# Banks of the s5 read-out and of the gelu's transposes taken from the heads' pool

## The chip, the cores and the metric

The kernel runs on one core of one Trainium2 chip. The metric is the device time of one execution in microseconds (us); lower is better. All times below are from that core.

## What is computed

One inference step of a decoder layer: 2,048 prompt tokens with 16 meta tokens ahead of them, and 8 single sampled tokens. The reference, cut to the part in which the change lies:

```python
def block(h, ...):
    hn = rms_norm(h, norm_mix_g)
    z = hn @ w_in
    u, q, fl, iv, g = ...
    y5, s5r, s5i = s5_mix(u, ...)
    yh, hg = hgrn_mix(q, fl, iv, g, ...)
    h = h + jnp.concatenate([y5, yh], axis=-1) @ w_out
    yf, conv = conv_ffn(rms_norm(h, norm_ffn_g), ...)
    return h + yf, ...

def s5_mix(u, ...):
    xr = jnp.einsum('nlgc,gpc->nlgp', ug, bbr)
    xi = jnp.einsum('nlgc,gpc->nlgp', ug, bbi)
    ...
    _, _, hr, hi = lax.associative_scan(_complex_scan_op, (a_r, a_i, xr, xi), axis=1)
    y = (jnp.einsum('nlgp,gcp->nlgc', hr, c_re) - jnp.einsum('nlgp,gcp->nlgc', hi, c_im))
    y = y.reshape(n, l, S5_DIM) + d * uf
    y = jax.nn.gelu(y)
    y = y * jax.nn.sigmoid(y @ w_glu + b_glu)
    return y, hr[:, -1], hi[:, -1]
```

`hgrn_mix` is a gated linear recurrence of four heads in chunks of 64 tokens; its matrix state goes from chunk to chunk.

## The kernel before

The prompt is cut into four blocks of 512 tokens (b = 0 to 3); the meta and sampled tokens ride with block 0. Dense products are made in three passes of split fp32 (high and low parts of weights and activations): `fm_mm` (matmul L480) for features by tokens, `tm_mm` (L500) for the heads' v and gate, `tm_wide` (L520) for the output projection. Each weight unit is loaded by SP into `st`, split by ACT (`wh`, L449) and DVE (`wl`, L83), two stages and three splits deep.

For each block `head` runs for h = 0 to 3: the forget gate's projection (L480), a running product and its reciprocal on DVE, q's projection, v and gate (L500), then the attention of the head on PE: scores (L723), transposed keys (L729), state increments (L734), output (L746, L747), with the state update on DVE between (L743, L80). The transposes of the finished head (L768, in `tail`) are put off to the next head by the list `PEND`, which `flush` empties after the next projection. After the heads, `u_proj` projects u, which goes to DRAM and comes back in the layout of s5 as tile `U` (by SP, L839, and, for the tokens of block 0's extras, by POOL, L842 and L845).

The s5 mixer of block b - 1 runs in eight units `bt`, two ahead of each head of block b (four ahead of the first two heads of the last block). A unit's chain is: increments on PE (L896) into a bank `tp`; a swap of its halves by ACT (L272, L273) and products on DVE (L86, L80); a scan on DVE (L934); swap, products and a subtraction again (L86, L83); the read-out on PE (L948, with the direct part L945 on U), copied by ACT into `sY` (L954). Units of block 0 also carry the extra tokens: L906, L919 to L929, L960, L963, L968. After the second unit of a pair, `s5_finish` (put off through `PEND` as well) makes the gelu (L86, L853, ACT L855, L856), transposes it on PE (L863, L872) and splits it (ACT L866, DVE L867).

PSUM has eight banks of 128x512 fp32, in three pools: `ps` with three (`bank`, name `mm`), `pt` with two (`tbank`, name `tp`), `pg` with three (`gbank`, name `hg`). A tile framework orders the instructions of each engine: it gives out a pool's banks in the order in which the program asks for them, and an instruction whose bank isn't free yet comes later in its engine's queue. So the pool that a bank comes from decides what may be placed ahead of what. In the program's order a pair of units asks first (increments, read-out), then the flush inside the head (tail of the head before, finish of the pair), then the head's scores, keys and increments.

Of the kernel before, what the change touches and what calls it, by code (L numbers as in the profile page):

```python
# [37 lines left out]
def kernel(  # L38
# [52 lines left out]
    def tbank():  # L91
        return pt.tile([128, 512], F32, name="tp")

    def gbank():
        return pg.tile([128, 512], F32, name="hg")
# [14 lines left out]
    def v3(t, a, b):  # L110
        return t[:, :a * b].rearrange("p (a b) -> p a b", a=a)
# [374 lines left out]
    def behind(ins, prev):  # L486

        if prev is not None:
            tc.add_manual_dep(ins.ins, prev.ins.name, mybir.DependencyInfo(
                mybir.DependencyClass.NoSync, mybir.DependencyReason.DATA), reason="bank shared by groups")  # L490
        return ins
# [88 lines left out]
    def put_cols(a, src, ks, lo, n):  # L580

        hi = a[0][:, ks, lo:lo + n]
        nc.vector.tensor_copy(hi, src)
        sub(a[1][:, ks, lo:lo + n], src, f_(hi))
# [263 lines left out]
    def gelu2(y, m):  # L848

        q = s5p.tile([128, 516], F32, name="sB")[:m, :512]  # L850
        yy = y[:m]
        mul(q, yy, yy)
        ts_(q, q, 0.044715, 1.0, op0=OP.mult, op1=OP.add)  # L853
        mul(q, q, yy)
        ACT(q, q, AF.Tanh, scale=GELU_C)  # L855
        stt(yy, q, 1.0, yy, op0=OP.add, op1=OP.mult)  # L856

    def s5_finish(b, bt, Y, ye, m):
        ft = bt // 2
        gelu2(Y.rearrange("p a b -> p (a b)"), 128)  # L860
        p = v3(tbank(), 4, 128)
        for t in range(4):
            nc.tensor.transpose(p[:, t, :], Y[:, t, :], ident)  # L863
        hi = m[0][:, 4 + ft, 0:BT].rearrange("p (j t) -> p t j", t=4)
        lo = m[1][:, 4 + ft, 0:BT].rearrange("p (j t) -> p t j", t=4)
        ACT(hi, p, AF.Copy, scale=0.5)  # L866
        stt(lo, p, 0.5, f_(hi), op0=OP.mult, op1=OP.subtract)  # L867
        if b == 0:
            gelu2(ye.rearrange("p a b -> p (a b)"), 9)
            p = v3(tbank(), 3, 16)  # L870
            for i, t in enumerate((0, 2, 3)):
                nc.tensor.transpose(p[:, i, 0:9], ye[:9, t, :], ident[:9, :9])  # L872
            tm = sm.tile([128, 10], F32, name="yx", bufs=2)
            ts_(tm[:, 0:2], p[:, 1:3, 0], 0.5, None, op0=OP.mult)
            ts_(tm[:, 2:10], p[:, 0, 1:9], 0.5, None, op0=OP.mult)
            put_cols(m, tm[:, None, :], slice(4 + ft, 5 + ft), FM_, 10)

    def s5(b, ut, m, bts, later=None):
        for bt in bts:
# [59 lines left out]
            mul(Gw, Gw, St)  # L939
            sub(G, G, Gw)  # L940
            nc.vector.tensor_copy(Hc[:, 4 * bt:4 * bt + 4], G[:, :, 128])
            py = v3(tbank(), 4, 64)
            o = None
            for i in range(2):
                behind(mm(py[:, 2 * i:2 * i + 2, :].rearrange("p a b -> p (a b)"), UT[:, i, 0:128], T[:, i, :],  # L945
# [8 lines left out]
            ACT(Y[:, :, 64 * half:64 * half + 64].rearrange("p t (g c) -> p g t c", c=16),  # L954
                py.rearrange("p g (t c) -> p g t c", c=16), AF.Copy)
            if b == 0:
                pye = v3(tbank(), 4, 64)
                o = None
                for i in range(2):
                    behind(mm(pye[:9, 2 * i:2 * i + 2, :].rearrange("p a b -> p (a b)"),  # L960
                              UT[:, i, 131:140], T[:, i, :], start=True, stop=False), o)
                    for j in range(2):
                        o = mm(pye[:9, 2 * i:2 * i + 2, :].rearrange("p a b -> p (a b)"), he[:, 2 * i + j, :],  # L963
                               Cm[:, 2 * i + j, :], start=False, stop=(j == 1))
                if half == 0:
                    E["ye"] = s5p.tile([128, 4, 128], F32, name="sY")
                ye = E["ye"]
                ACT(ye[:9, :, 64 * half:64 * half + 64].rearrange("p t (g c) -> p g t c", c=16),  # L968
                    pye[:9].rearrange("p g (t c) -> p g t c", c=16), AF.Copy)
            if half == 1:  # L970
                fin = lambda m, bt=bt, Y=Y, ye=E.get("ye"): s5_finish(b, bt, Y, ye, m)
                if later is None:
                    PEND.append(lambda fin=fin: fin(m))
                else:
                    later.append(fin)
# [119 lines left out]
    for b in range(NB):  # L1095
# [4 lines left out]
        for h in range(4):  # L1100
            if last and h == 2:
                U[b] = u_proj(b, A[b])
                fin = []
                stage_out(b - 1, lambda q: s5(b, U[b], None, (q,), fin))
                M[b] = new_act(b)
                mix_split(b, M[b], MIX[b])
                for f in fin:
                    f(M[b])
            if last and h < 2:
                s5(b - 1, U[b - 1], M[b - 1], range(4 * h, 4 * h + 4))  # L1110
            elif last:
                s5(b, U[b], M[b], (2 * h, 2 * h + 1))
            elif b > 0:
                s5(b - 1, U[b - 1], M[b - 1], (2 * h, 2 * h + 1))
            MIX[b].append(head(b, A[b], h))
            if b == 0 and h == 0:
                s5_factors()
                setup = s5_setup()
                next(setup)
            if b == 0 and h == 1:  # L1120
                next(setup, None)
            if b == 0 and h == 2:
                norm1(1)
# [234 lines left out]
```

## Time and profile before

| what | us |
|---|---|
| median of 3 runs (2536.32 to 2539.64) | 2537.81 |
| the profiled execution | 2535.7 |
| its span, first to last instruction | 2534.0 |
| PE busy in it | 2445.5 |
| DVE busy in it | 1453.3 |
| ACT busy in it | 902.6 |

Busy time is the union of an engine's instructions; that of PE holds the overlapping tails of matmuls that follow each other. The times of the rows below count from the span's start. The heads and s5 take about the first 1,000 us, the ConvFFN the rest.

### The profile page before, as it was taken

What the parts mean: (1) busy time and instruction counts of PE and PEld (TensorE: products, weight loads), DVE (VectorE), ACT (ScalarE), POOL (GpSimd) and SP (SyncE); (2) the same over time, 40 slices, a digit from 0 to 9 for tenths busy, and PEclk for the clock granted to TensorE, in tenths of its full rate; (3) what the DMA queues carried; (4) which work ended last, traced back from release to release, by engine and by line L of the source; (5) the groups of instructions that cost most, each with busy time, mean ns of one, the idle gap of its engine ahead of it and who ended that gap; (6) DMA issues with size and microseconds to landing.
All of it is one profiled execution on the core that took longest, in us unless ns stands there. A gap on an engine that the chain in (4) does not pass through costs nothing.

```text
span 2534.0 us, 33854 instructions
## 1 busy us (share of the span) xinstructions
PE 2445.5 (97%) x13515; PEld 2088.5 (82%) x13515; DVE 1453.3 (57%) x2950; ACT 902.6 (36%) x1548; POOL 166.6 (7%) x252
## 2 busy tenths in 40 slices
PE   7989899999999989999999999999999999999998
PEld 6878787788888778888989898988788888888886
DVE  6897788688678688553343434445843433343344
ACT  3554445344435444432313131323531313131222
POOL 2223001000100001000000000000400000000000
PEclk9999999999999999999999999999999999999999
DMA  4357435543564555531111111111621111111112
GB/s 126 103 159 205 114 101 141 191 142 127 148 215 158 162 164 192 170 92 43 50 44 48 47 45 42 46 55 59 211 66 50 44 48 50 50 50 50 34 54 80
DMA packets 251260, 252.13 MB, mean 99 GB/s; under 512 B 11303, under 2 KB 208751, under 8 KB 246998
## 3 DMA queue, kind: packets, MB, share of 16 engines
q1 hardware_dynamic: 241088, 220.42, 28.8%
q0 software_dynamic: 9840, 29.48, 3.6%
q8 instruction: 106, 1.74, 0.3%
q14 instruction: 52, 0.43, 0.1%
q10 hardware_dynamic: 174, 0.06, 0.0%
HBM read 216.41 MB, written 33.27 MB: 99 GB/s over the span
## 4 chain that ended last, share of the span: by engine, by line
PE 72%; DVE 11%; issue 4%; ACT 3%; DMA 1%; POOL 1%; SPq 0%; POOLq 0%; ACTq 0%; DVEq 0%
PE mm L480 42%; PE mm L1282 9%; PE hg L1282 9%; PE mm L500 3%; PE hg L520 3%; PE mm L520 2%; DVE sB L86 2%; DVE sA L934 1%; DVE wl L83 1%; DVE sA L86 1%; PE mm L539 1%; DVE hf L665 1%; POOL rstd L546 1%; DMA x<-h_d 1%; PE tp L572 1%
## 5 line engine op out<-in xcount | busy, mean ns | idle before, releaser
L480 PE MATMUL mm<-ah,wh 128*128 128x512 f32 (+3 forms) x2312 | 811.6, 351 | 5.9 <-ACT ah L577 3.3
L480 PE MATMUL mm<-al,wh 128*128 128x512 f32 (+3 forms) x2312 | 810.8, 351 | 1.1 <-DVE al L83 1.1
L480 PE MATMUL mm<-ah,wl 128*128 128x512 f32 (+3 forms) x2312 | 810.8, 351 | 1.0 <-DVE wl L83 1.0
L449 ACT ACTIVATE wh<-st 128x1024 fp32r<-128x1024 f32 (+1 forms) x264 | 276.4, 1047 | 709.2 <-PE mm L480 298.0
L83 DVE TENSOR_TENSOR wl<-st,wh 128x1024 fp32r<-128x1024 f32 (+1 forms) x264 | 318.4, 1206 | 350.4 <-ACT wh L449 348.4
L480 PEld LDWEIGHTS mm<-ah,wh 128*128 128x128 f32 x2312 | 438.9, 190 | 59.7 <-ACT ah L577 3.9
L480 PEld LDWEIGHTS mm<-ah,wl 128*128 128x128 f32 x2312 | 438.7, 190 | 56.2 <-issue 1.6
L480 PEld LDWEIGHTS mm<-al,wh 128*128 128x128 f32 x2312 | 438.1, 189 | 54.8 <-DVE al L83 1.6
L86 DVE TENSOR_TENSOR c<-c,mm 128x512 f32<-128x512 f32 (+1 forms) x110 | 63.6, 580 | 211.7 <-PE mm L480 210.3
L500 PE MATMUL mm<-wh,ah 128*128 128x256 f32 x512 | 146.3, 286 | 3.0 <-DVE hP L86 1.7
L500 PE MATMUL mm<-wl,ah 128*128 128x256 f32 x512 | 144.8, 284 | 1.7 <-DVE wl L83 1.7
L500 PE MATMUL mm<-wh,al 128*128 128x256 f32 x512 | 145.9, 285 | 0.0
L1282 PE MATMUL mm<-wh,gh 128*128 128x512 f32 x352 | 137.4, 390 | 0.0
L1282 PE MATMUL hg<-wh,gl 128*128 128x512 f32 x352 | 137.1, 390 | 0.0
L1282 PE MATMUL hg<-wl,gh 128*128 128x512 f32 x352 | 137.1, 390 | 0.0
L1282 PE MATMUL mm<-wh,gl 128*128 128x512 f32 x352 | 137.1, 389 | 0.0
L1282 PE MATMUL mm<-wl,gh 128*128 128x512 f32 x352 | 137.1, 389 | 0.0
L1282 PE MATMUL hg<-wh,gh 128*128 128x512 f32 x352 | 137.0, 389 | 0.0
L80 DVE TENSOR_TENSOR hacc<-hacc,hg 128x512 f32<-128x512 f32 x96 | 65.8, 686 | 88.2 <-PE hg L1282 87.7
L1220 ACT ACTIVATE c<-c 128x512 f32<-128x512 f32 x88 | 55.6, 632 | 144.8 <-DVE c L1219 144.8
L80 DVE TENSOR_TENSOR hacc<-hacc,mm 128x512 f32<-128x512 f32 x96 | 65.7, 685 | 66.0 <-PE mm L1282 65.8
L500 PEld LDWEIGHTS mm<-wh,ah 128*128 128x128 f32 x512 | 97.7, 191 | 4.7 <-DVE hP L86 2.5
(406 smaller groups left out, 3569.0 us busy)
## 6 DMA issues: line engine op xcount, KB each, us to landing
st<-in_ffn_w_up_dram SPq DMA_DIRECT2D x96, 512.0 KB, 3.8
big<-tab_d SPq DMA_DIRECT2D x32, 1156.0 KB, 5.4
st<-in_w_in_dram SPq DMA_DIRECT2D x48, 512.0 KB, 5.0
st<-in_ffn_w_down_dram SPq DMA_DIRECT2D x40, 512.0 KB, 3.5
st<-in_w_in_dram SPq DMA_DIRECT2D x64, 256.0 KB, 3.1
st<-in_w_out_dram SPq DMA_DIRECT2D x32, 512.0 KB, 3.6
x<-in_x_prompt_dram SPq DMA_DIRECT2D x30, 512.0 KB, 5.0
h_d<-x POOLq DMA_DIRECT2D x16, 512.0 KB, 4.2
```

What stands on the lines that cost most here:

```text
L80: tt_(o, a, b, op=OP.add)
L83: tt_(o, a, b, op=OP.subtract)
L86: tt_(o, a, b, op=OP.mult)
L449: ACT(hi[:, :n], st[:, :n], AF.Copy)
L480: mm(p[:, :n], w[wi][:, k, :], a[ai][:, k, c0:c0 + n], start=(i == 0), stop=(i == 3 * nk - 1))
L500: o = mm(dst, lhs(ai, k), (hi, lo)[wi][:, kk, :], start=(i == 0), stop=(i == tot - 1))
L520: mm(pb[t], lhs(ai, k, t), wu[wi][:, kk, :], start=(k == 0 and j == 0), stop=(k == 7 and j == 2))
L539: mm(dst[:m], stat[:, k, :m], w[:, kk, :], start=(i == 0), stop=(i == tot - 1))
L546: nc.gpsimd.tensor_tensor(r, r, mhalf[:ss.shape[0], :n], op=OP.pow)
L572: nc.tensor.transpose(p[:, k, :], x[:, kk * 128:kk * 128 + 128], ident)
L1220: ACT(c, c, AF.Silu)
L1282: mm(ps_[t], gs[b, f0 + k][ai][:, t * 128:t * 128 + 128], wus[i][wi][:, kk, :], start=(k == 0 and j == 0), stop=(k == nf - 1 and j == 2))
```

## The change

The read-out banks (`py`, and `pye` of block 0's extra tokens) and the two banks of the gelu's transposes come from `pg`, the pool of the heads' attention, in place of `pt`. The increments keep `pt` for themselves.

```diff
     def s5_finish(b, bt, Y, ye, m):
         ft = bt // 2
         gelu2(Y.rearrange("p a b -> p (a b)"), 128)
-        p = v3(tbank(), 4, 128)
+        p = v3(gbank(), 4, 128)
         for t in range(4):
             nc.tensor.transpose(p[:, t, :], Y[:, t, :], ident)
...
             gelu2(ye.rearrange("p a b -> p (a b)"), 9)
-            p = v3(tbank(), 3, 16)
+            p = v3(gbank(), 3, 16)
...
-            py = v3(tbank(), 4, 64)
+            py = v3(gbank(), 4, 64)
...
             if b == 0:
-                pye = v3(tbank(), 4, 64)
+                pye = v3(gbank(), 4, 64)
```

What it does to the order of the queues is shown at three places.

PE at the first head of block 1, before: after the last L500 of head 0 the head's attention follows, then the next projection (mm_3084 is the bank of head 0's v and gate, hP and hk its decayed queries and keys).

```order
L500 MATMUL mm_3084<-wl_3028,ah_1734 128x256
L723 MATMUL hg_3135<-hP_2968,hk_2966 128x128 x4
L729 MATMUL hg_3143<-ident_111,hk_2966 128x128 x4
L746 MATMUL mm_3154<-hv_3031,att_3140 128x128
L747 MATMUL mm_3154<-Sp_3155,hP_2968 128x128
L734 MATMUL hg_3149<-hv_3031,hf_2935 128x128 x4
L746 MATMUL mm_3154<-hv_3031,att_3140 128x128
L480 MATMUL mm_3340<-ah_1734,wh_3336 128x512
```

The same place now (big_2756 is the table of unit 0, big_2831 that of unit 1; sA holds a unit's scan, he its extra states):

```order
L500 MATMUL mm_3084<-wl_3028,ah_1734 128x256
L896 MATMUL tp_2760<-U_2472,big_2756 128x148 x2
L896 MATMUL tp_2761<-U_2472,big_2756 128x148 x2
L945 MATMUL hg_2813<-big_2756,U_2472 128x128
L960 MATMUL hg_2822<-big_2756,U_2472 9x128
L945 MATMUL hg_2888<-big_2831,U_2472 128x128
L896 MATMUL tp_2835<-U_2472,big_2831 128x148 x2
L896 MATMUL tp_2836<-U_2472,big_2831 128x148 x2
L963 MATMUL hg_2822<-big_2756,he_2799 9x128 x2
```

and, after the read-out matmuls of both units, the end of this piece:

```order
L948 MATMUL hg_2888<-big_2831,sA_2833 128x128 x2
L896 MATMUL tp_3190<-U_2472,big_3186 128x148 x2
L896 MATMUL tp_3191<-U_2472,big_3186 128x148 x2
L863 MATMUL hg_2943<-ident_111,sY_2820 128x128 x4
L872 MATMUL hg_2956<-ident_111,sY_2829 128x9 x3
L723 MATMUL hg_3135<-hP_2968,hk_2966 128x128 x4
```

Units 0 and 1, which stood behind the head's attention, stand whole ahead of it, with their finish, and no row of L480 or L500 lies between.

PE at the first head of block 3, now (before, L863 of units 2 and 3 stood 16 L480 matmuls further on, inside the next projection):

```order
L500 MATMUL mm<-wl,ah 128x256
L896 MATMUL tp<-U,big 128x128 x2
L863 MATMUL hg<-ident,sY 128x128 x4
L948 MATMUL hg<-big,sA 128x128 x2
L945 MATMUL hg<-big,U 128x128
L948 MATMUL hg<-big,sA 128x128 x2
L896 MATMUL tp<-U,big 128x128 x2
L863 MATMUL hg<-ident,sY 128x128 x4
L723 MATMUL hg<-hP,hk 128x128 x4
```

The first L863 is the finish of units 0 and 1, the second that of units 2 and 3, whose last read-out stands two matmuls ahead of it.

PE in the output projection of block 3's stretch, where the first units of block 3 begin, now:

```order
L520 MATMUL mm<-wl,ah 128x512
L896 MATMUL tp<-U,big 128x128 x4
L945 MATMUL hg<-big,U 128x128
L896 MATMUL tp<-U,big 128x128 x4
L945 MATMUL hg<-big,U 128x128
L520 MATMUL hg<-wh,ah 128x512
```

Then come 18 rows of L520 in all, and L948 of the first of the two units. Before, 37 rows of L520 lay between its L896 and its L948, and the second unit's L896 stood after the first eight of them.

## Rows read from the trace of the kernel before

**Rows 1.** The page: span, busy time of PE and DVE, their 40 slices.
```profile
span 2534.0 us, 33854 instructions
...
PE 2445.5 (97%) x13515; PEld 2088.5 (82%) x13515; DVE 1453.3 (57%) x2950; ACT 902.6 (36%) x1548; POOL 166.6 (7%) x252
...
PE   7989899999999989999999999999999999999998
...
DVE  6897788688678688553343434445843433343344
```

**Rows 2.** Windows from head to head: length, busy us (x), PEclk, DMA, GB/s.
```profile
259.10:305.60 46.50, 40.22 (x250) 33.61 (x250) 32.58 (x93) 19.05 (x48) 1.58 (x2) 0.93 0.32 89
305.60:345.90 40.30, 38.42 (x258) 32.34 (x257) 35.21 (x106) 20.36 (x51) 1.53 (x2) 1.00 0.36 114
...
385.80:440.90 55.10, 51.99 (x323) 42.43 (x321) 44.60 (x123) 32.55 (x73) 7.17 (x10) 1.00 0.53 148
...
596.10:630.80 34.70, 33.34 (x230) 29.80 (x229) 30.56 (x66) 15.72 (x31) 1.65 (x2) 1.00 0.41 130
630.80:669.60 38.80, 38.33 (x195) 32.23 (x193) 19.28 (x34) 18.49 (x35) 5.29 (x8) 1.00 0.48 115
```

**Rows 3.** PE's waits, whole span: us in total, times, longest.
```profile
PE tp L948 <- DVE sA L83: 5.2, 12, 1.0
PE tp L945 <- DVE sB L86: 4.0, 7, 1.1
PE tp L945 <- ACT pe L906: 3.7, 5, 2.3
PE tp L945 <- DVE al L867: 3.3, 2, 2.6
...
PE mm L480 <- ACT wh L449: 2.2, 1, 2.2
```

**Rows 4.** Timeline of PE at block 1's first head: start, us.
```profile
259.05 1.05 PE L723 MATMUL hg<-hP,hk 128*128 128x128 f32 x8
259.94 0.60 PE L729 MATMUL hg<-ident,hk 128*128 128x128 f32 x4
```

**Rows 5.** Timeline of POOL, the last of U's transfers.
```profile
256.40 0.56 POOL L845 DMA_DIRECT2D U<-udx  x1 [0.41 <-DMA U<-udx]
```

**Rows 6.** DMA issues by tile: count, KB, median us to landing.
```profile
U<-udx POOLq DMA_DIRECT2D x8, 4.0 KB, 7.3
```

**Rows 7.** Timeline of PE, unit 1 of block 0.
```profile
292.36 1.27 PE L896 MATMUL tp<-U,big 128*128 128x148 f32 x8
...
303.88 0.71 PE L948 MATMUL tp<-big,sA 128*128 128x128 f32 x4 [0.34 <-DVE sA L83]
...
310.34 0.60 PE L863 MATMUL tp<-ident,sY 128*128 128x128 f32 x4
```

**Rows 8.** Timeline of DVE, the same unit.
```profile
295.80 0.17 DVE L86 TENSOR_TENSOR mx<-pe,big 128x16 f32<-128x16 f32 x1
...
297.32 0.18 DVE L86 TENSOR_TENSOR mh<-mg,big 128x20 f32<-128x20 f32 x1
...
298.77 0.17 DVE L931 COPY sA<-Hc 128x4 f32<-128x4 f32 x1
...
303.97 1.22 DVE L83 TENSOR_TENSOR wl<-st,wh 128x1024 fp32r<-128x1024 f32 x1
```

**Rows 9.** Timeline of PE, two matmuls of the output projection.
```profile
875.12 0.39 PE L520 MATMUL hg<-wl,ah 128*128 128x512 f32 x1
875.34 0.39 PE L520 MATMUL hg<-wh,ah 128*128 128x512 f32 x1
```

**Rows 10.** PE's waits from 833.4 to 927.5 us, block 3's output projection and third head.
```profile
PE tp L945 <- DVE al L867: 2.6, 1, 2.6
PE tp L896 <- DMA big<-tab_d: 2.4, 1, 2.4
PE tp L863 <- DVE sY L856: 1.3, 2, 0.8
PE tp L945 <- DVE sB L86: 1.1, 1, 1.1
```

## The prediction

> **What bounds the kernel now.** I read the page first [rows 1]: TensorE (PE) is busy 97% of the span and at 9 tenths in 35 of the 40 slices, VectorE (DVE) 57%, but 6 to 9 tenths in the first 16 slices, where the heads, s5 and projections run. So time is won or lost only where PE stands still, and it stands still only in the first 1,050 us. Then the windows from head to head [rows 2]: with two s5 units per head PE is idle 6.3 us between the first two heads of block 1 (46.5 less 40.22), 1.9 in the next stage, 3.1 in the last, 1.4 in a stage of block 2. DVE is at 35.21 of 40.3 us in the second stage. The same last stage in block 2, which holds no s5 unit, has 0.5 us idle. Then the list of PE's waits [rows 3]: the first read-out matmul L945 waits 4.0 + 3.7 + 3.3 = 11.0 us in all, mostly for a reader of the increments (L86, L906) to give a bank of `pt` back; L948, which waits for the scan's result and not for a bank, 5.2 us. Behind a waiting matmul PE runs nothing else: that idle time is PE's own, with L480 or L500 queued behind.
>
> **What the change does to order.** No instruction is added or removed; a pair of units now takes six banks of pool `pg` in block 0's s5 and three later. L945 no longer shares two banks with L896, and the three banks of `pg` are now handed from s5 to head and back in the program's order: py, pye, py, pye of a pair, the finish, then pa, pk, kv of the head. So a head's attention now stands behind the read-out and the finish of the pair ahead of it. The order shows it: at the first head of block 1, PE's queue goes from the last L500 straight into units 0 and 1 and their transposes, and only then to L723.
>
> **Term A, the stand at the first head of block 1.** PE comes there at 259.05 [rows 4]. L896 needs U. The last of U's small transfers is issued on POOL at 256.40 [rows 5] and such a one takes 7.3 us to land [rows 6]: 263.7, or 4.7 us of standing. Unit 1 of the trace shows one chain nearly undisturbed: L896 starts at 292.36, L948 at 303.88 [rows 7]: 11.5 us. In the changed DVE order two weight splits (1.22 us each [rows 8]) and about 2 us of unit 1's early work lie inside unit 0's chain, some of it beside the swaps on ACT: 13.5. Unit 1's scan stands behind unit 0's last subtraction; from the small state work ahead of the scan to L948 this is the stretch from 297.32 to 303.88 in the trace [rows 7, 8], 6.6 us. Then its read-out matmuls, the copy and the gelu up to L863: from 303.88 to 310.34 in the trace [rows 7], 6.5 us, of which 1.2 us is a weight split that isn't there now and 0.4 the second half's; I take 5.3, and 1.5 us for the finish transposes until L723. Sum 4.7 + 13.5 + 6.6 + 5.3 + 1.5 = 31.6, so L723 begins near 290.7 and not at 259.05. In it PE does work that it did later before: a group of four 128-column fp32 matmuls takes 0.89 us (L723 to L729 [rows 4]), that is 0.22 each; 28 of these, 12 L896 of 148 columns at 0.25 (a quarter of 1.27 us without its last 0.27 [rows 7]), and three tiny ones make 9.5 us. Idle anew: **+22**. Ends: with U 2 us earlier and the units overlapped fully, 15; with both chains end to end, 28.
>
> What hides it: nothing. PE's queue has no stream between L500 and L723 there. In the trace of before the cover was head 0's attention and 24 L480 matmuls, then some 50 L480 and L500 around unit 0.
>
> **Term B, what the last stage of the block gives back.** The last pair is now read out before head 3's attention, so the projection of u behind it (and the glu) runs as 168 L480 in a row. The stage with units idles 3.1 us, the one without 0.5 [rows 2]. A record of PE is longer than the spacing (0.39 against 0.23 us [rows 9]), so each interruption hides up to 0.16 us more; with some 15 interruptions: **-5** (ends -2.5 and -7).
>
> **Term C, the rest of the first stage.** The waits for a weight split (2.2 us) and for pe (longest 2.3 us) that the 6.3 idle us hold [rows 2, 3] go, as both splits are made during the stand. Against that, unit 2's L948 now stands only 13 L480 (3 us) behind the attention while DVE still has the head's state update, unit 2's scan and unit 3's increments to do. **-2** (ends -4.4 and +4).
>
> **Term D, block 2.** L945's three waits there, 0.6 us each, go; but L948 waits for the same DVE chain, so most of it comes back one row later. The first pair now has both units' L896 together, with 48 L480 (10.8 us) to cover two chains. **-1** (ends -4 and +4).
>
> **Term E, block 3.** New: at the first head L863 of units 2 and 3 stands two matmuls behind L948 with L723 behind it: copy, five gelu steps, so the 5.3 us above without the second half's 0.6 and with PE's own 1.1 and 0.4 taken off, **+3.2**. At the second head 17 L500 (2 us) cover the same: **+1.5**. In the output projection the first pair's L948 stands 18 L520 (4.1 us) and some 1.3 us of small matmuls behind its L896; a unit without block 0's extra state takes the 11.5 us less the stretch from 295.80 to 298.77 [rows 8] except 0.6 us of it, 9.1: **+3.7**. Gone, as the rows stand further apart: the wait for a table, 2.4, half of the wait of L945 for al, 1.3, the waits for sB and sY, 1.1 + 1.3 [rows 10]: **-6.1**. Together **+2** (ends -6 and +10).
>
> The same work on ACT, POOL and the DMA queues is issued as before. SP's table loads stand in other places, three in a row at two points; weights queued behind them are asked for only after the reads that free the tables, so I cost this at nothing, and at up to 3 us inside E's upper end if that cover is gone.
>
> **Sum.** 22 - 5 - 2 - 1 + 2 = +16 us on the profiled execution's 2535.7 us; its span is 2534.0 [rows 1]. The median of the runs shown is 2.1 us above it, so I expect 2537.8 + 16 = **2554 us**.
>
> The Trainium skill speaks against this sum: "Perfetto Trace Analysis", Optimization Strategy, says that the same gap repeating on the engine that should be saturated can mean too little SBUF or PSUM for the next tile. By it L945's repeated waits [rows 3] are the thing to cure, and curing them is worth 11.0 us: 2527. The trace agrees that these waits are for banks; it also shows that the cover the heads gave to s5 is worth more.
>
> **Rivals.** *Faster:* L945's 11.0 us of waits end, and the stand A is small, because DVE, free of the head's work, runs both chains far quicker than in the trace. Price at A near 0: 2537.8 - 11 = 2527. It decides if PE stands less than about 9 us between the last L500 of head 0 and L723; for it speaks only that these waits are real, against it that U alone costs 4.7 and the scan's chain 6.6. Chance 0.05. *Given back:* DVE paces block 1 (87% of the second stage) and does some 18 us of s5 during the stand, so the three later stages lose nearly all of their idle time, 13 us with B and the hidden part: +5, 2543. Against it: each later stage still holds two units, as before. Chance 0.13. *Heavier:* the low clock that [rows 2] show (0.93 granted in the stage that holds such a pause; a drop to 1.2 GHz) returns for longer after the stand, and C and E come out at their upper ends: 28 - 2.5 + 4 + 9 = +38, about 2576 at worst, 2567 in the middle. Chance 0.14. That the change leaves the order alone is excluded by the rows of the order.
>
> **Chances.** Forecast 0.68 (+8 to +24, 2546 to 2562), the rivals 0.05, 0.13, 0.14. The range 2541 to 2567 takes in most of the second rival and half of the third; about 0.18 lies outside. What a measurement of this kernel tells from no change is 0.2%, 5.1 us: faster 0.06 (the first rival and a tail), same 0.11 (most of the second), slower 0.83.
>
> **What would show it.** In the changed profile: L723 of block 1's first head near 290 and PE idle in 15 to 28 us of the stretch before it; L945's waits nearly gone, L948's grown; the stage after head 3 of block 1 shorter by some 5 us; waits of L863 for sY at the first two heads of block 3. Wrong, if PE runs L480 or L500 inside that stretch, if it reaches L723 before 270, or if the stages after it are shorter by more than 10 us together.

## The result and the profile after

The changed kernel takes 2567.55 us (median of 4 runs, 2563.3 to 2570.93); the kernel before, beside it, 2538.72 (4 runs, 2536.32 to 2539.99). The ratio is 1.0114, 95% interval 1.0096 to 1.0131: slower by 28.8 us. The direction was forecast, the size was not: +16 was expected (2554 us), and the measured time lies just above the range that was given (2541 to 2567). The profiled execution is the longest of the four, 2570.93 us.

The page after, its lines that answer to [rows 1]:

```profile
span 2569.2 us, 33880 instructions
...
PE 2461.7 (96%) x13515; PEld 2113.4 (82%) x13515; DVE 1456.2 (57%) x2950; ACT 902.5 (35%) x1548; POOL 167.0 (7%) x252
...
PE   7989699999997999999999999999999999999998
...
DVE  6786696698678588554433334344943434343344
```

VectorE (DVE) and ScalarE (ACT) do the same work in the same time; TensorE (PE) falls from 8 tenths to 6 in the fifth slice and from 9 to 7 in the thirteenth, where block 1's first head and block 3's first two heads run. The windows, with the columns of [rows 2] (length, busy us of PE, PEld, DVE, ACT, POOL, PEclk, DMA, GB/s): from block 0's last head to block 1's first, the four stages after it, a stage of block 2 with units, and from the output projection of block 1 over the first two heads of block 3 to the next output projection.

```profile
205.30:304.90 99.60, 77.90 (x485) 66.68 (x483) 63.90 (x178) 43.28 (x112) 23.85 (x40) 0.85 0.70 181
304.90:344.70 39.80, 38.71 (x249) 33.25 (x250) 33.97 (x106) 17.74 (x43) 1.95 (x2) 0.95 0.22 76
344.70:383.30 38.60, 37.12 (x258) 32.30 (x257) 35.27 (x105) 19.96 (x50) 1.53 (x2) 1.00 0.40 129
383.30:422.70 39.40, 37.23 (x259) 32.42 (x258) 36.53 (x108) 20.40 (x50) 3.04 (x4) 1.00 0.36 114
422.70:462.30 39.60, 39.12 (x242) 34.85 (x241) 20.35 (x43) 18.49 (x39) 5.54 (x8) 1.00 0.50 119
617.70:653.00 35.30, 33.12 (x231) 29.95 (x230) 30.74 (x66) 15.76 (x31) 1.56 (x2) 1.00 0.40 127
692.10:785.90 93.80, 84.03 (x460) 71.58 (x459) 74.03 (x131) 39.26 (x59) 4.03 (x6) 0.97 0.66 205
785.90:831.20 45.30, 39.64 (x266) 36.01 (x266) 38.99 (x87) 21.11 (x40) 2.49 (x3) 0.95 0.34 119
831.20:872.40 41.20, 40.51 (x187) 34.10 (x186) 18.57 (x31) 16.29 (x29) 4.38 (x7) 0.92 0.51 135
```

The last three have these lengths in the trace of before:

```profile
669.60:749.80 80.20, 78.93 (x434) 66.42 (x432) 61.85 (x111) 32.80 (x50) 4.04 (x6) 1.00 0.64 194
749.80:789.40 39.60, 36.57 (x254) 32.58 (x252) 36.58 (x80) 20.28 (x38) 2.44 (x3) 1.00 0.50 167
789.40:833.50 44.10, 42.98 (x224) 35.50 (x224) 32.48 (x59) 23.25 (x42) 4.36 (x7) 1.00 0.64 185
```

Together they took 163.9 us and take 180.3: +16.4, in a part for which the prediction had next to nothing. DVE's busy time in them is the same (130.9 and 131.6 us), but in the first two, where PE waits for it, it is 113.0 and not 98.4.

The list of PE's waits over the whole span (us, times, longest), against [rows 3]:

```profile
PE hg L948 <- DVE sA L83: 22.0, 19, 3.9
PE hg L863 <- DVE sY L856: 13.1, 7, 4.5
...
PE tp L896 <- issue: 5.9, 1, 5.9
PE hg L963 <- DVE he L928: 5.4, 3, 3.4
PE tp L896 <- DMA big<-tab_d: 4.0, 3, 3.1
...
PE hg L945 <- DVE al L867: 1.3, 1, 1.3
```

L945's 11.0 us are down to 1.3, as the change promises. What stands in their place is longer: L948 22.0 instead of 5.2, L863 13.1.

**The first block is not part of it.** Up to block 0's last head no row of the order differs. That head's L723 came at 196.1 us before and at 205.3 in the profiled execution of the change, but at 197.0 and at 195.6 in two runs below that have the change for nearly all or all units. In the 205.3 us the three stages ahead of it have a granted clock of 0.87, 0.92 and 0.90; in the 196.1 us it is 0.97, 0.96 and 1.00. So the start moves from execution to execution with PE's clock, and stages are compared by their length here.

### The profile page after: what moved, and what is told of

Same layout as the page of the kernel before. It is cut to its first block, busy times and chain, and to the rows that moved or that the text cites. A ratio compares the mean times of both kernels' runs of the same rounds, so it can differ in the third digit from the quotient of the medians.

```text
span 2569.2 us, 33880 instructions
## 1 busy us (share of the span) xinstructions
PE 2461.7 (96%) x13515; PEld 2113.4 (82%) x13515; DVE 1456.2 (57%) x2950; ACT 902.5 (35%) x1548; POOL 167.0 (7%) x252
## 4 chain that ended last, share of the span: by engine, by line
PE 74%; DVE 10%; DMA 3%; ACT 2%; issue 2%; POOL 1%; SPq 0%; POOLq 0%; ACTq 0%; DVEq 0%
PE mm L480 42%; PE mm L1282 9%; PE hg L1282 9%; PE mm L520 3%; PE hg L520 3%; PE mm L500 3%; DVE sA L934 1%; DVE sB L86 1%; DVE sA L86 1%; DVE hf L665 1%; PE tp L896 1%; PE mm L539 1%; PE hg L948 1%; DMA st<-in_w_in_dram 1%; DVE wl L83 1%
## 5 line engine op out<-in xcount | busy, mean ns | idle before, releaser
L480 PE MATMUL mm<-ah,wh 128*128 128x512 f32 (+3 forms) x2312 | 810.5, 351 | 3.9 <-ACT ah L577 3.5
L480 PE MATMUL mm<-al,wh 128*128 128x512 f32 (+3 forms) x2312 | 810.4, 351 | 1.1 <-DVE al L83 1.1
L480 PE MATMUL mm<-ah,wl 128*128 128x512 f32 (+3 forms) x2312 | 809.0, 350 | 0.0
L480 PEld LDWEIGHTS mm<-ah,wh 128*128 128x128 f32 x2312 | 439.3, 190 | 58.5 <-ACT ah L577 4.1
L480 PEld LDWEIGHTS mm<-ah,wl 128*128 128x128 f32 x2312 | 439.4, 190 | 55.1 <-issue 1.2
L480 PEld LDWEIGHTS mm<-al,wh 128*128 128x128 f32 x2312 | 438.9, 190 | 54.9 <-DVE al L83 1.6
L500 PE MATMUL mm<-wh,ah 128*128 128x256 f32 x512 | 147.5, 288 | 2.7 <-DVE hP L86 1.8
L500 PE MATMUL mm<-wl,ah 128*128 128x256 f32 x512 | 146.4, 286 | 0.0
L500 PE MATMUL mm<-wh,al 128*128 128x256 f32 x512 | 146.3, 286 | 0.0
L500 PEld LDWEIGHTS mm<-wh,ah 128*128 128x128 f32 x512 | 98.9, 193 | 4.0 <-DVE hP L86 2.6
```

Source lines behind the costliest of these rows:

```text
L480: mm(p[:, :n], w[wi][:, k, :], a[ai][:, k, c0:c0 + n], start=(i == 0), stop=(i == 3 * nk - 1))
L500: o = mm(dst, lhs(ai, k), (hi, lo)[wi][:, kk, :], start=(i == 0), stop=(i == tot - 1))
```

## Block 1: the stand, as predicted

PE at block 1's first head (start, us), against [rows 4]:

```profile
273.13 2.31 PE L896 MATMUL tp<-U,big 128*128 128x148 f32 x8 [5.90 <-issue]
...
284.24 1.02 PE L963 MATMUL hg<-big,he 128*9 128x128 f32 x4 [3.42 <-DVE he L928]
...
289.30 1.22 PE L948 MATMUL hg<-big,sA 128*128 128x128 f32 x4 [2.76 <-DVE sA L83]
...
297.21 0.71 PE L948 MATMUL hg<-big,sA 128*128 128x128 f32 x4 [2.21 <-DVE sA L83]
...
303.46 1.12 PE L863 MATMUL hg<-ident,sY 128*128 128x128 f32 x4 [3.86 <-DVE sY L856]
...
304.93 1.43 PE L723 MATMUL hg<-hP,hk 128*128 128x128 f32 x5
```

The parts of term A can be read off: the wait for U 5.9 us (4.7 expected; the row names no releaser, but the last of U's transfers was issued on POOL at 263.59, and they take 4.8 to 9.6 us to land), unit 0 from L896 to L948 16.2 (13.5), unit 1 7.9 (6.6), the gelu to L863 6.3 (5.3), the finish 1.5 (1.5). The chains and the gelu are some 20% longer than expected. One reason is in the rows: the same group of four L948 matmuls takes 1.22 us in unit 0 and 0.71 eight us later in unit 1. The granted clock is 0.50, the lower level of 1.2 GHz, from 271.6 to 295.5, which begins while PE stands for U:

```profile
271.60:295.50 23.90, 14.24 (x54) 9.99 (x54) 14.60 (x55) 10.88 (x29) 0.00 (x0) 0.50 0.30 92
```

## The experiments

### Which units carry the loss

Three runs give the banks of `pg` to some blocks' units alone; `b` in `s5` is the block that the units belong to; they run beside block b + 1.

```diff
-            py = v3(gbank(), 4, 64)
+            py = v3((gbank if b == 0 else tbank)(), 4, 64)
```

(and so for `pye` and the two banks of `s5_finish`; the second run has `b > 0`, the third `b == 2`.)

Block 0's units alone:

> The banks come from pg only for block 0's units (those that run in block 1); the units of blocks 1 to 3 take them from pt as before. PE's order is that of the changed kernel until block 2 and that of the one before from there. Order theory (the time lies in PE standing where units are put whole ahead of a head's attention): L723 of block 1's first head near 305, block 1 +12 us against before, block 3 as before (L863's waits there gone): 2538.7 + 12 = 2551, if the 10 us that the first block lost at an unchanged order are chance, and 2561, if they go with the change. Rival (what the low clock costs in the first block and in block 3 follows any long stand): 2561 or more, with block 3 over 320 us. By the terms of the prediction, A + B + C alone: 2554.

Measured: 2552.62 us, 1.0058 (1.0043 to 1.0073), +14.8. L723 of the first head came 99.4 us after block 0's last, the three stages of block 3 took 163.8.

All but block 0's:

> The banks come from pg only for the units of blocks 1 to 3. PE's order is that of the one before through block 1 and that of the changed kernel from block 2 on. Order theory: L723 of block 1's first head near 260 again, block 2 within 2 us, block 3 some 13 us longer with L863 waiting 4 to 5 us at each of its first two heads: 2538.7 + 14 = 2553. By the terms D and E of the prediction: 2540. Rival (the long stand in block 1 is what disturbs the clock and the table loads later): block 3 within 3 us of before, 2541.

Measured: 2552.82 us, 1.0058 (1.0041 to 1.0074), +15.0. Block 1 as before; block 2 1.5 us longer; the three stages of block 3 181.7.

Block 2's alone:

> The banks come from pg only for block 2's units (those that run beside block 3's first two heads); all others from pt as before. Theory (all of the loss that the terms D and E missed is made at those two heads, by the work of four units being put ahead of each attention): L723 of block 3's first head 14 us later against the output projection before it, the second stage 6 us longer, the third 3 us shorter: 2537.4 + 17 = 2554. Rival (the loss is spread: block 2's stages and block 3's own units carry a third of it or more): 2549 or less.

Measured: 2555.83 us, 1.0075 (1.006 to 1.009), +20.6 on the 2535.2 of the kernel before beside it. The three stages took 179.7 us.

The first two add up to +29.8, the change's +28.8 within the intervals. Block 1 costs the 15 us that A + B + C gave; D + E cost 15 and not 1; and that is made by block 2's units at block 3's first heads (179.7 us there instead of 163.9). Block 3's own units gain: 2.8 us from the output projection on (last run below), so block 2's units alone should cost some 16 (15.0 + 2.8 - 1.5); the +20.6 has an interval of 15 to 23.

### Does the stand go where the order puts it

Units 0 and 1 of block 0 keep their banks of `pt`; the order then has units 2 and 3 whole ahead of block 1's second head.

```diff
-            py = v3(gbank(), 4, 64)
+            py = v3((gbank if not (b == 0 and bt < 2) else tbank)(), 4, 64)
```

(and so for `pye` and the two banks of `s5_finish`.)

> The changed kernel, but units 0 and 1 of block 0 take their banks from pt as before; all others from pg. PE's order then has units 2 and 3 with their finish whole ahead of the attention of block 1's second head. Order theory: the first head's L723 comes near 260, the stand is at the second head, without the 5 us of U's landing but with both chains: 15 to 22 us there, so 2567.6 - 5 = 2562. Rival (the stand is U's arrival and the first unit's start after the block's change, not the order): the second head stands under 8 us, and the time is 2550 or less.

Measured: 2571.21 us. The first head's L723 came at 259.7, and the stage after it grew from 46.5 us to 83.1; of that, 9.8 is PE's own work moved there (by the spacing of the rows), so PE loses 26.8 us more:

```profile
259.70:342.80 83.10, 59.63 (x337) 47.87 (x335) 58.96 (x173) 35.53 (x89) 1.58 (x2) 0.81 0.35 107
```

The rival (only U's arrival) falls. The price was too low: 15 to 22 was expected, and a table's load (4.4 us, for an L945) and the low clock (0.81 over the stage) came on top.

Now the pools of the change, with the units asked for behind the head:

```diff
+            run = None
...
-                s5(b - 1, U[b - 1], M[b - 1], (2 * h, 2 * h + 1))
+                run = lambda h=h: s5(b - 1, U[b - 1], M[b - 1], (2 * h, 2 * h + 1))
             MIX[b].append(head(b, A[b], h))
+            if run is not None:
+                run()
```

(and so for the four units ahead of the last block's first two heads.)

> The changed kernel with its pools, but the program asks for a pair of units after the head and not ahead of it (s5 is called behind head, for the pairs of blocks 0 and 1 and for those of block 2 in the last block). No unit stands whole ahead of an attention in blocks 1 and 2; two pairs still do at block 3's second head. Order theory (pg itself costs nothing, the order of asking does): L723 of block 1's first head near 260, the waits of L945 gone, block 1 shorter than before by 5 to 10 us, block 3 about as in the changed kernel less half its loss: 2532 to 2540. Rival (three banks of pg are too few for heads and read-out together, in whatever order): L948, L863 and L723 wait at every head and the time stays over 2555.

Measured: 2542.13 us, 1.0015 (1.0004 to 1.0025), 2 us above the range given. From block 1's first L723 to its L520 it takes 175.7 us; before, 181.8. So in block 1 `pg` shared by heads and read-out costs nothing; who asks first decides. It loses at block 3's first heads, where the three stages take 69.7, 52.4 and 52.1 us, 174.3 together and not 163.9 (four units still stand ahead of the second head, and units have moved from the first stage into the others), and in block 2: 231.2 us and not 228.7. No unit stands whole ahead of a head there, and L948 waits 7.9 us and not 2.3. That `pg` costs nothing in whatever place is therefore not shown.

### What stands at block 3's heads

PE and DVE in the changed kernel at block 3's first head:

```profile
775.84 0.68 PE L896 MATMUL tp<-U,big 128*128 128x128 f32 x4 [3.09 <-DMA big<-tab_d]
...
778.60 1.06 PE L948 MATMUL hg<-big,sA 128*128 128x128 f32 x4
...
784.97 1.12 PE L863 MATMUL hg<-ident,sY 128*128 128x128 f32 x4 [4.54 <-DVE sY L856]
```

```profile
780.11 0.69 DVE L86 TENSOR_TENSOR sB<-sY 128x512 f32<-128x512 f32 x1 [0.51 <-ACT sY L954]
780.84 0.43 DVE L853 TENSOR_SCALAR sB<-sB 128x512 f32<-128x512 f32 x1
781.69 0.69 DVE L86 TENSOR_TENSOR sB<-tp,big 128x512 f32<-128x512 f32 x1 [0.42 <-ACT sA L273]
782.29 0.68 DVE L86 TENSOR_TENSOR sB<-sB,sY 128x512 f32<-128x512 f32 x1
782.89 0.68 DVE L86 TENSOR_TENSOR sA<-sA,big 128x512 f32<-128x512 f32 x1
783.61 0.69 DVE L80 TENSOR_TENSOR sB<-sB,sA 128x512 f32<-128x512 f32 x1
784.22 0.69 DVE L856 SCALAR_TENSOR_TENSOR sY<-sB,sY 128x512 f32<-128x512 f32 x1
```

Three things: an L896 waits for its table; between the gelu's DVE steps (780.11, 780.84, 782.29, 784.22) stand three products of the next unit (781.69, 782.89, 783.61), some 0.6 us each; and the clock falls behind the wait (a group of L948 takes 1.06 us; at 755.36 in the same view, 0.61). The finish's banks alone back in `pt`, for block 2's units:

```diff
-        p = v3(gbank(), 4, 128)
+        p = v3((gbank if b != 2 else tbank)(), 4, 128)
```

> The changed kernel, but the two banks of the finish of block 2's units (those that run in block 3) come from pt again; their read-out and all else from pg. In PE's order no L863 and no third unit's L896 stands ahead of L723 at block 3's first head, and no L863 of the last pair at its second. Theory (E is the finish put ahead of the attention, with the table wait and the low clock that follow it): the stages before the first and the second head of block 3 fall from 93.7 and 45.3 us to about 82 and 41, so 2567.6 - 15 = 2553. Rival (E comes from the read-out's banks shared with the heads): the two stages stay over 90 and 44 us, 2563 or more.

Measured: 2561.34 us, 1.0097 (1.0083 to 1.0111). Neither theory: the first stage is 80.5 us, as said, but the second rose:

```profile
684.60:765.10 80.50, 78.29 (x434) 66.56 (x432) 61.94 (x111) 32.44 (x48) 4.04 (x6) 1.00 0.64 198
765.10:816.00 50.90, 42.02 (x274) 38.09 (x273) 43.05 (x94) 22.73 (x43) 2.13 (x3) 0.93 0.40 135
816.00:861.30 45.30, 41.72 (x205) 34.51 (x204) 25.70 (x45) 20.68 (x37) 4.36 (x7) 0.96 0.54 161
```

In the second and third stage L896 waits 3.9 us for tables, and L734, L768, L948 and L746 1.7 to 1.9 each for ACT and DVE. The converse, read-out in `pt`, finish in `pg` (`py = v3((gbank if b != 2 else tbank)(), 4, 64)`):

> The converse: the read-out of block 2's units takes its banks from pt again, their finish from pg. PE's order still has the third unit's L896 and both finishes ahead of L723 at block 3's first head. Theory as for the run with the finish in pt: L863 waits 4 to 5 us there, twice, and the time stays at 2564 to 2570. Rival: 2553.

Measured: 2560.31 us: the stages take 90.6, 45.3 and 39.5. L863 waits 8.0 us as expected, no table is waited for. The time lies between theory and rival: either half of the change alone costs some 12 us in these three stages, the whole 16.

Then the loads of four tables left out:

```diff
-            tab = bigt()
-            dma_w(tab[:, :TB], tab_d[bt])
+            if b == 2 and bt % 2:
+                tab = E["tab"]
+            else:
+                tab = E["tab"] = bigt()
+                dma_w(tab[:, :TB], tab_d[bt])
```

> The changed kernel, but the odd units of block 2 use the table of the even unit ahead of them, which is loaded once: the loads of four tables are left out, and the output of those units is another. Theory: the wait of L896 for its table at block 3's first head (3.3 us) goes, and the low clock behind it with it or in part, but L863's waits stay: the first stage of block 3 takes 87 to 90 us and not 93.7, the time is 2561 to 2564. Rival (the table is the whole of it; L863 is late only because its unit's table was): the first stage takes 82 us or less, the time is 2555 or less.

Measured: 2567.04 us, above the range given. The first stage takes 87.4, in the range said; the second takes 54.1 instead of 45.3, with L863 and a weight split (4.1 us) waited for and a granted clock of 0.84. Its order is not the same at that head, so the run prices the table at the first head only. Three times a removed wait let the stand come out elsewhere. That points to what the waits share, DVE's queue, but doesn't show it. So its load was changed. First, the weight splits of the two heads on POOL (`E["pool"]` is set for these heads alone):

```diff
-        sub(lo[:, :n], st[:, :n], f_(hi[:, :n]))
+        if E.get("pool"):
+            nc.gpsimd.tensor_tensor(lo[:, :n], st[:, :n], f_(hi[:, :n]), op=OP.subtract)
+        else:
+            sub(lo[:, :n], st[:, :n], f_(hi[:, :n]))
```

> The changed kernel, but the weight splits of block 3's first two heads (four of each, 1.22 us each on DVE) are made by POOL, which takes 2 us for the same elements in another place. Theory (DVE is what those stages wait for: its queue holds the units' products and the splits in a row): DVE loses 10 us of work in the two stages, the stages lose 4 to 8 us: 2560 to 2563. Rival (the waits are chains through ACT, PE and the tables' loads, and DVE's load is not what counts): unchanged or longer, 2567 or more.

Measured: 2577.25 us, 9.7 slower than the change itself. By the expectation's own reading the rival; but the rows show that DVE was not relieved. A row of POOL's timeline and, at the same place, three of DVE's (line numbers lie three further on there: L859 is L856):

```profile
777.30 5.16 POOL L451 TENSOR_TENSOR wl<-st,wh 128x1024 fp32r<-128x1024 f32 x2 [13.12 <-ACT wh L449]
```

```profile
776.78 0.69 DVE L86 TENSOR_TENSOR sB<-sB,big 128x516 f32<-128x516 f32 x1
777.51 2.73 DVE L83 TENSOR_TENSOR sA<-sA,sB 128x516 f32<-128x516 f32 x1
780.16 2.84 DVE L859 SCALAR_TENSOR_TENSOR sY<-sB,sY 128x512 f32<-128x512 f32 x1
```

Two DVE instructions, of a kind that takes 0.69 us, took 2.7 and 2.8 beside POOL's two: DVE stood while they ran. The eight splits took 2.44 us each on POOL against 1.22 on DVE, so DVE had up to 9.8 us more to get through, not 10 less. The other way leaves the splits out (`E["skip"]` is set for the same heads):

```diff
         ACT(hi[:, :n], st[:, :n], AF.Copy)
+        if E.get("skip"):
+            return hi, hi
         sub(lo[:, :n], st[:, :n], f_(hi[:, :n]))
```

> The changed kernel without the low parts of the weights in block 3's first two heads: the eight splits L83 there (1.22 us each on DVE, 10 us in all) are left out and the low part's matmuls read the high part instead, so those heads' output is another; PE's work is the same. Theory (those stages wait for what stands in DVE's queue; with the splits on POOL every DVE instruction that met one took as long as POOL's, so DVE had about 10 us more, and the time was 10 us more): the first two stages of block 3 lose 6 to 10 us, 2558 to 2562. Rival (the waits are the chains of copy, gelu and table load alone): the two stages stay within 3 us of 93.7 and 45.3, 2565 or more.

Measured: 2560.81 us (1.0087, 1.0063 to 1.0112), in the range of the theory, 6.7 below the change, with eight splits of 1.22 us gone from DVE's queue:

```profile
686.60:775.60 89.00, 82.44 (x460) 70.02 (x459) 65.43 (x122) 38.76 (x59) 4.03 (x6) 0.99 0.69 216
775.60:820.50 44.90, 38.57 (x266) 34.92 (x266) 39.90 (x88) 21.02 (x40) 2.29 (x3) 0.98 0.38 131
820.50:859.60 39.10, 37.49 (x187) 31.45 (x186) 18.25 (x30) 16.11 (x29) 4.38 (x7) 1.00 0.49 131
```

The first two stages lost 5.2 us and not 6 to 10; the third, whose clock was 0.92 and is 1.00, 2.1. L896's wait for tables fell from 4.1 to 0.2 us, which fits tables that came late because their predecessors were read late. L863's waits stayed (8.6 us), and the three stages are still 9.1 us longer than before, so DVE's load is a part of the loss and not the whole. Some matmuls stand in another order here too, so the split of the 7 us is not exact.

### Does the low clock follow the stand

```diff
+            if b == 0 and bt < 2:
+                q = last
+                for j in range(70):
+                    w = mm(tbs[1][:, 296:512], A[1][0][:, j % 8, 0:128], A[1][0][:, j % 8, 0:216], start=(j == 0), stop=(j == 69))
+                    q = behind(w, q)
```

(`tbs` are the two increments' banks, `last` the last L896; `behind` puts one matmul behind another in PE's queue.)

> The changed kernel with work added: 70 matmuls of 216 columns on the first head's activations, written to the unused columns of the increments' bank, stand in PE's queue behind L896 of unit 0 and 70 more behind that of unit 1, where PE stood (about 0.1 us each, 14 us in all; nothing reads them, the output is unchanged). Theory (the low clock, 23.9 and 6.8 us of it in that stage in the changed kernel, follows PE's standing, and costs 9 to 11 us there): the clock stays at its upper level for most of the stretch, the added work lies in idle time, L723 comes at most 2 us later against block 0's last L723, or earlier by up to 6 us: 2561 to 2568. Rival (the low clock comes on its own, or with the load of that stretch): it is granted as before and the stage is 8 us or more longer, 2576.

Measured: 2578.27 us, by the number the rival. But the added work was not in idle time: ACT's swap of the same bank waited 6.8 and 6.0 us for the last of the added matmuls, so they lay in the chain itself, and the time says nothing of the clock. The rows do:

```profile
262.00:268.80 6.80, 3.93 (x17) 3.96 (x18) 1.11 (x2) 2.53 (x5) 0.00 (x0) 0.50 0.25 53
268.80:285.90 17.10, 12.41 (x103) 11.15 (x102) 9.07 (x30) 4.37 (x13) 0.00 (x0) 1.00 0.22 62
```

PE had stood 6.1 us ahead of the first L896, and the clock fell to 0.50. PE then ran 9 us of added work without a pause (from 266.8 on); within it, at 268.8, the clock rose to its upper level and stayed there to 285.9, where the changed kernel has 0.50 for 23.9 us. From 299.6 on it is 0.50 again for 17.1 us, of which PE is busy 8.5. That fits a clock that follows PE's standing; no run fills the stand without lengthening it, so it is not settled.

### A version that beats both

```diff
+            py = v3((gbank if b in (0, 3) else tbank)(), 4, 64)
...
-                s5(b - 1, U[b - 1], M[b - 1], (2 * h, 2 * h + 1))
+                run = lambda h=h: s5(b - 1, U[b - 1], M[b - 1], (2 * h, 2 * h + 1))
+                if b > 1:
+                    run = run()
             MIX[b].append(head(b, A[b], h))
+            if run is not None:
+                run()
```

> A version put together from the runs: banks from pg for the units of blocks 0 and 3 alone, and those of block 0 asked for behind the head, not ahead of it. By the stages of the runs: block 1 as in the run with all pairs behind the head, 6 us shorter than before, the second half of block 3 as in the changed kernel, 2.8 us shorter, all else as before: 2537.8 - 9 = 2529. Rival (each stage's gain is given back in the next, as DVE's work is the same): 2535 or more.

Measured: 2529.83 us against 2537.0, ratio 0.997 (0.9959 to 0.9982): 7 us faster than the kernel before. From block 1's first L723 to its L520 it is 4.9 us shorter (6 was expected). The three stages at block 3's first heads are those of before, at full clock (the third takes 44.0 us):

```profile
667.10:747.20 80.10, 78.85 (x433) 66.41 (x431) 61.66 (x111) 32.55 (x50) 4.03 (x6) 1.00 0.64 193
747.20:786.90 39.70, 36.67 (x254) 32.67 (x253) 36.69 (x80) 20.39 (x38) 2.44 (x3) 1.00 0.49 167
```

From its output projection on, block 3 is 2.8 us shorter than before, about as in the changed kernel (2.9). The run takes two steps at once, and none has the asking moved with all banks left in `pt`: how much of block 1's gain needs `pg` is not shown.

## Why the prediction was right or wrong

**The mechanism in block 1 was right.** Banks are given in the order of asking, so units stood whole ahead of an attention; the run with units 0 and 1 kept in `pt` moved the stand to the next head, and the run with the units asked for behind the head removed it. The first head's L723 was expected some 32 us late; it came 37 late (99.6 us after block 0's last head instead of 62.9).

**A, B and C: right in sum, and in part by luck.** In the profiled execution A is +27.7 instead of +22 (36.7 us longer, of which some 9.0 is work moved there), B -6.5 instead of -5, C -6.7 instead of -2, and the two stages between, for which nothing was put, -2.2: +12.3. The run with block 0's units alone gave +14.8, the prediction +15. So 5.7 us missing in A and 8.4 too few given back behind it nearly cancel. A sign that was named as "Wrong" came with it: the stages after the stand are shorter by 15.4 us together, and more than 10 was to count against the sum. A was too small, in part by its low clock; in C PE idles 1.1 us of the stage (6.3 before [rows 2]), and the waits that were set against the gain did not come.

**D: a small miss.** +1.5 in the run without block 0's units, -1 expected: PE idles 2.2 us in a stage of block 2 and not the 1.4 of [rows 2]. L945's waits in block 2 went (2.1 us), and L948's rose from 2.3 to 6.5: more came back than went.

**E failed.** The step was "Together +2": from the output projection of block 1 to that of block 3 it took 312.8 us before and takes 326.3 in the profiled execution, +13.5. It failed in three terms.

- "+3.2" and "+1.5" for L863 at the two heads: measured 4.5 and 3.8. The gelu's steps were priced as if DVE had nothing else; three products of the next unit stand between them. At the second head the 2 us of cover came to nothing: products of the head itself and a weight split of 1.21 us stand between the gelu's steps there.
- "I cost this at nothing" for the tables: measured 3.5 and 0.6. The third table is asked for at 770.6, only when PE's L948 has read the one whose place it takes (from 770.0 on; a like L948 just ahead had waited 0.6 us for DVE's subtraction), and its L896, which waits until 775.8, now stands ahead of L723. The 3 us named as an upper end, should the cover go, were about right; the cover was gone. DVE had 15 us more to do in these two stages, and without the weight splits the wait is 0.2 us.
- No term for the clock in E. At 0.50 PE was busy 3.4 + 5.4 + 6.1 us in the rows below, 14.9 us of work. By the clock alone half of that, 7.5 us, is lost: an estimate, and an upper bound, since part of it may run beside DVE's work that PE waits for. In the trace of before these stages have 1.00 throughout.

```profile
776.80:780.20 3.40, 3.40 (x18) 3.20 (x15) 2.63 (x5) 1.48 (x2) 0.00 (x0) 0.50 0.53 156
783.60:790.40 6.80, 5.43 (x26) 5.44 (x27) 5.05 (x10) 2.95 (x6) 0.00 (x0) 0.50 0.10 41
831.40:838.20 6.80, 6.11 (x28) 5.62 (x27) 3.71 (x7) 2.60 (x3) 0.00 (x0) 0.50 0.51 151
```

The misses are 3.6 + 4.1 + at most 7.5 = 15.2 us; E missed by 11.5. The difference of 4 us was not traced: the clock can have cost less, and small waits went. L948 in the output projection waits 3.9 us (3.7 expected). Two of the prediction's own subtractions are off by some tenths, which changes little: in A 6.5 less 1.2 and 0.4 is 4.9 and not 5.3, and in E 3.2 less the cover of 2 is 1.2 and not 1.5.

**The rivals.** *Heavier* had the time in its middle (2567) and named the low clock and E's upper end (+10; +13.5 came); it put C at its upper end too, and C came out lower than the forecast. Its chance of 0.14 was too small, since the clock was tied to the stand alone, though here it also fell behind the new waits at block 3's heads. *Given back* had about the size of what came back behind the stand (13 us put, 15.4 measured), but A was larger and E came on top. *Faster* fell: L945's waits ended, and the time rose. The Trainium skill ("Perfetto Trace Analysis", Optimization Strategy) says that a gap which repeats on the engine that should be saturated can mean too little PSUM for the next tile. The rows agree that L945 waited for banks, 11.0 us before and 1.3 after, but that counts only the waits that go and not the ones that a new order brings.

## What to carry to other kernels

Where banks are given in the order of asking, a pool shared by two streams is an ordering rule: price it by who is put ahead of whom, and look at the order of asking before moving the banks. A chain that is moved ahead of a barrier is priced by everything in the other engine's queue at that place, not by its own instructions; if that engine is already at 92% of the stage (36.6 of 39.6 us here), what is moved there came out as waiting, and taking one wait away showed it at the next head. Put a term for the half speed beside each new pause of PE: here stretches of 3.4 to 23.9 us at 0.50 came with waits of 3.1 to 5.9 us.

## What was not expected of the hardware

A two-input POOL instruction (2.44 us on average) held a DVE instruction beside it for nearly its whole length (2.73 us and not 0.69), so POOL was no place to unload DVE to. The Trainium skill says so ("SBUF — State Buffer", SBUF: two separate sides): the ports that the two share are an exclusive lock for the whole instruction; the rows agree. PE's clock also differed between executions in a stretch with the same instructions: block 0's last head began at 195.6 to 205.3 us.
